# A hybrid attention and DeltaNet layer on one core: scan operands loaded in portions, scales folded into a matrix, pauses in the late modulation

## The chip, the cores and the metric

The kernel runs on one core of a Trainium2 chip. Its engines are TensorE (PE; its weight loads are listed apart as PEld), VectorE (DVE), ScalarE (ACT), GpSimd (POOL) and SyncE (SP), which here only issues transfers. Each engine takes its own instructions in order and waits for the others through semaphores. The metric is the device time of one execution in microseconds (us); lower is better. Times are medians of several runs, and one further run is made under the profiler.

## The reference

One layer over 256 latent tokens and 256 context tokens of width 2048, all in float32. Cut to what matters here:

```python
sh1, sc1, g1, sh2, sc2, g2 = split(silu(c) @ w_ada + b_ada, 6)      # modulation of the latents
p_l = modulate(rmsnorm(x, norm_mix), sh1, sc1) @ w_in               # the same for ctx with c_ctx
k, v = mla_kv(...)      # rmsnorm, w_kv_b; rmsnorm of [k_nope, k_rope] over 192; rotary on k_rope
q = mla_q(...)          # rmsnorm, w_q_b; rmsnorm over 192 with weight q_norm; rotary on the last 64
y_mla = softmax(q @ [k_l, k_c].T * 192**-0.5) @ [v_l, v_c]          # 8 heads
# DeltaNet, per head and direction, 8 chunks of 64: 4 of the context, then 4 of the latents
v_new = u_c - w_c @ s;  s_next = s * g_c + k_c.T @ v_new            # the scan over chunks
o = q_c @ s + a_c @ v_new                                           # latents only
y = sigmoid(ga) * (y_mla @ w_o_mla) + sigmoid(gb) * (y_dn @ w_o_dn)
x = x + g1 * (y @ w_out)
x = x + g2 * conv_glu(modulate(rmsnorm(x, norm_ffn), sh2, sc2), w_ffn_up, ffn_conv, w_ffn_down)
```

The modulation has six parts. The kernel calls the first two early (they are needed at once) and the other four, `g1`, `sh2`, `sc2`, `g2`, late.

## The kernel before, in words

Activations lie transposed, 128 features on the partitions and 256 tokens of a stream along a row. To keep accuracy, a weight tile `raw` (128 x 1024, 512 KB) is split into two halves: `split` lets ACT write the rounded value `whi` (L119) and DVE the rest `wlo` (L120), 512 columns at a time. `mm_hl` then does two matmuls: `whi` against both parts of the activation (512 columns) and `wlo` against its high part (256 columns). There are NR=5 buffers of `raw` and NH=6 pairs of `whi` and `wlo`. All PE work is issued through one helper, so that its rows have line L68.

The stages, with their place in the profiled execution: the early modulation and first projections (0 to 152 us, names `fp`, `amp`); the DeltaNet head inputs (`mmp`, to 441); attention with the gates `wz` and `wgm` as filler (`kps`, `qps`, `sps`, `yps`, `gtp`, to about 757); the scan with the gates `wgd` and the attention's output projection as filler (`kp`, `yp`, `sp_`, `op`, `gtp`, `brp`, to 957); `o_norm` and the second output projection (`obp`, `brp`, to 1036); `wout` (`ops`, to 1127); the gated MLP's up projection (`fps`, to 1630); its down projection (`dps`, to 1874).

**The late modulation** is `ada_rest`, a generator of 128 steps. Each loads a tile `rawa` of 512 KB into the same five `raw` buffers, one step ahead, and lets DVE multiply it with `sch` and sum it (L271). `sch` is one half of silu(c), spread over the partitions and loaded from `Sc` in DRAM into its only buffer at steps 0, 16, 48, 80 and 112. `Side` gives a generator time: a caller adds nanoseconds to what is owed, and the generator runs until the costs that it yields (1300 for a step) have used them up. So its steps are spread over the stages by numbers: ADB in the head inputs, AD in the attention, ADS in the scan, WO for each of the 16 tiles of `wout`, 1000 for each of the 43 tiles of the up projection. Before `wout` the first of the four parts must be done, and after it the third (`while ada.done < 3: ada(1)`), since `h2_tile` needs `adaT` of both; `ada.finish()` stands ahead of the down projection.

**The scan** goes over 8 chunks in the order 4, 5, 6, 7, 0, 1, 2, 3; the last four also give the output. The state `S` depends on the step before: PE `kp`, DVE `r`, PE `yp`, ACT `y`, PE `sp_`, DVE `S`. Its operands are loaded by SP into `jit`, two buffers of each: `kt` (`KTs`), `v` (`Vs`), the inverted system `tt` (six transfers from `Xq` and `Xo`), `ke` (`KEs`). Steps with output load `av` (`As`, two transfers) and `qe` (`QEs`) too, with one buffer each.

**The attention** works on pairs of heads. `k_head` makes the keys `kps`, splits them into `kt` and squares them (`ksq`) for the norm `ks`; `q_tile` makes the queries `qx` and multiplies them by their norm weights; the third tile holds the rotary part, and `rps` multiplies it by the matrix `perm`, which swaps halves.

The scheduler that builds the program may move instructions of an engine against each other where nothing is pinned, so that the written order is not the issued one. Every transfer of SP and ACT takes one of eight completion semaphores in turn and waits for its last user.

Of the kernel before, what the change touches and what calls it, by code (L numbers as in the profile page):

```python
# [8 lines left out]
F32 = mybir.dt.float32  # L9
# [7 lines left out]
P = 128  # L17
# [19 lines left out]
CB = 2000  # L37
CC = 7000
RE = 1.0
ADS = 0.4  # L40
OD = 8000
OC = 4000
WO = 500
IK = 7000
NW = 3
SCP = (2, 5, 7)
# [7 lines left out]
def hybrid_block(ctx: ExitStack, tc: tile.TileContext, io, dbg=None):  # L54
# [136 lines left out]
    def row_bcast(pl, ps, r, n):  # L191

        row_spread(ps, row_diag(pl, r, n), n)

    class Rms:
# [18 lines left out]
        def finish(self, mul, out):  # L214
            n, pl = self.n, self.pl
            ms = pl.tile([P, 4], F32, tag="ms", name="ms", bufs=1)[:, :n]
            dve.tensor_scalar(out=ms, in0=self.ss[:, :n], scalar1=mul, scalar2=EPS, op0=ALU.mult, op1=ALU.add)
            rsq(pl, ms, ms, n)
            bc_ps = psa.tile([P, 512], F32, tag="aux", name="bc_ps")
            row_bcast(pl, bc_ps, ms, n)  # L220
            if out is not None:
                act.copy(out.rearrange("p a b -> p (a b)"), bc_ps[:, : n * P])
            return bc_ps
# [27 lines left out]
    def ada_rest():  # L251


        def load(i):
            w = wr.tile([P, GR], F32, tag="raw", name="rawa", bufs=NR)
            c, n = divmod(i, 32)
            sync.dma_start(w, io["wada2"][c, (n // 16 + c) % 2, n % 16])
            return w

        parts = ad.tile([P, 2, 16], F32, name="parts")  # L260
        half, ahead = None, load(0)
        for i in range(128):
            c, n = divmod(i, 32)
            h, j = (n // 16 + c) % 2, n % 16
            if h != half:
                half, sch = h, ad.tile([P, GR], F32, tag="sch", name="sch")
                sync.dma_start(sch, Sc[h])
            w = ahead
            if i < 127:
                ahead = load(i + 1)  # L270
            dve.tensor_tensor_reduce(out=w, in0=w, in1=sch, scale=1.0, scalar=0.0, op0=ALU.mult, op1=ALU.add, accum_out=parts[:, h, j : j + 1])  # L271
            if n == 31:
                cs = slice(16 * c, 16 * c + 16)
                dve.tensor_tensor(out=adaT[:, cs], in0=parts[:, 0], in1=parts[:, 1], op=ALU.add)
                dve.tensor_tensor(out=adaT[:, cs], in0=adaT[:, cs], in1=bada[:, 32 + 16 * c : 48 + 16 * c], op=ALU.add)
                ada.done = c + 1
            yield 1300
# [632 lines left out]
    dve.tensor_scalar(out=krf[0:64], in0=krd[0:64], scalar1=off["kn_r"][0:64], scalar2=None, op0=ALU.mult)  # L910
    rp = psa.tile([64, T], F32, tag="aux", name="rp")
    pe.matmul(rp, perm[0:64, 0:64], krf[0:64, 0], start=True, stop=True)
    rt = pn.tile([P, T], F32, name="rt")
    dve.tensor_tensor(out=rt[0:64], in0=rp, in1=sinT[0:64], op=ALU.mult)
    dve.tensor_tensor(out=krf[0:64, 0], in0=krf[0:64, 0], in1=cosT[0:64], op=ALU.mult)
# [43 lines left out]
    def mla_project(b):  # L959
# [5 lines left out]
        def k_head(h2):  # L965
            kps = psa.tile([P, 512], F32, tag="aux", name="kps")
            for k in range(4):
                mm3(kps, W(h2 * 512 + k * P), [lat[k][:, n] for n in range(2)], k == 0, k == 3)
            kt = pc2.tile([P, 2, 512], F32R, tag=f"kt{h2}", name="kt")
            split(kps, kt[:, 0], kt[:, 1])  # L970
            ksq = pc2.tile([P, 512], F32, tag="ksq", name="ksq", bufs=1)
            act.activation(ksq, kps, AF.Square)
            kts.append(kt)
            sqs.append(ksq)

# [25 lines left out]
        def q_tile(j):  # L1001
            ps = psa.tile([P, 512], F32, tag="aux", name="qps")
            for k in range(4):
                mm_hl(ps, P, W(j * 512 + k * P), qan_[:, k], k == 0, k == 3)
            qx = pc2.tile([P, T], F32, tag="qx", name="qx")
            gather(ps, P, qx)
            act.activation(qsq[:, j], qx, AF.Square)
            act.activation(qx, qx, AF.Copy, scale=qkn if j < 2 else off["qn_r"])
            return qx

        k_head(0)
# [18 lines left out]
        for _ in sc0:  # L1030
            pass
        for j in range(2):
            qx = q_tile(j)
            split(qx, qts[j][:, 0], qts[j][:, 1])
        for _ in sc1:
            pass
        yield 3500
# [3 lines left out]
        pe.matmul(rps, perm, qx, start=True, stop=True)  # L1041
        rq = ryx[:, 0]
        dve.tensor_tensor(out=rq, in0=rps, in1=sinT, op=ALU.mult)
        dve.tensor_tensor(out=qx, in0=qx, in1=cosT, op=ALU.mult)
        dve.tensor_tensor(out=qx, in0=qx, in1=rq, op=ALU.add)
        for h2 in range(2):
            hs, ls = slice(64 * h2, 64 * h2 + 64), slice(64 - 64 * h2, 128 - 64 * h2)
# [130 lines left out]
    def scan():  # L1178
# [6 lines left out]
        S = ps1.tile([P, HEADS, 2, P], F32, name="S")  # L1185
        steps = (4, 5, 6, 7, 0, 1, 2, 3)

        def load(n):
            st = steps[n]
            kt, ke, v = (jit[:, 2 * j + n % 2].rearrange("p (h c) -> p h c", c=P) for j in range(3))  # L1190
            tt = TTv[n % 2]
            sync.dma_start(kt, KTs[st])
            sync.dma_start(v, Vs[st])
            for d in range(2):
                for r, c, x in ((0, 0, Xq[1]), (32, 32, Xq[2]), (0, 32, Xo)):
                    rs, cs = slice(64 * d + r, 64 * d + r + 32), slice(64 * d + c, 64 * d + c + 32)
                    n = 16 * d + 2 * st
                    sync.dma_start(tt[rs, :, cs], x[n : n + 2].rearrange("a g c i -> c (a g) i"))
            sync.dma_start(ke, KEs[st])
            return kt, ke, v, tt  # L1200

        def load_out(st):
            av = TTv[2]
# [4 lines left out]
            sync.dma_start(qe, QEs[st])  # L1208
            return av, qe

        ahead = load(0)
        yield 0
        for n, st in enumerate(steps):
            kt, ke, v, tt = ahead
            lat, first, last = st < 4, n == 0, n == 7
            if not last:
                ahead = load(n + 1)
            if lat:
                av, qe = load_out(st)
            rs = []  # L1220
            for q in range(2):
                if first:
                    rs.append(v[:, 4 * q : 4 * q + 4])
                    continue
                r = ps1.tile([P, 4, P], F32, tag="r", name="r", bufs=2)
                kp = psa.tile([P, 4, P], F32, tag="aux", name="kp")
                for j in range(4):
                    h = 4 * q + j
                    for d in range(2):
                        hs = slice(64 * d, 64 * d + 64)  # L1230
                        pe.matmul(kp[hs, j], kt[:, h, hs], S[:, h, d], start=True, stop=True)
                    dve.scalar_tensor_tensor(out=r[:, j], in0=kp[:, j], scalar=negc[:, st, h : h + 1], in1=v[:, h], op0=ALU.mult, op1=ALU.add)
                rs.append(r)
            yield CA
            y = ps1.tile([P, HEADS, P], F32, tag="y", name="y")
            for q in range(2):
                h4 = slice(4 * q, 4 * q + 4)
                yp = psa.tile([P, 4, P], F32, tag="aux", name="yp")
                for j in range(4):
                    pe.matmul(yp[:, j], tt[:, 4 * q + j], rs[q][:, j], start=True, stop=True)  # L1240
                act.copy(y[:, h4], yp)
            yield CB
            if lat:
                op = [psm.tile([P, 4, 2, 64], F32, tag="mm", name="op") for q in range(2)]
# [283 lines left out]
```

## Time and profile before

| what | value |
|---|---|
| median of 3 runs | 1875.42 us (1861.37, 1875.42, 1878.97) |
| profiled execution, its own time | 1875.89 us |
| its span, first to last instruction | 1874.0 us |
| granted TensorE clock, mean over the span | 0.983 |
| busy: PE, PEld | 1798.7 us (96%), 1533.5 us (82%) |
| busy: DVE, ACT, POOL | 1379.9 us (74%), 935.1 us (50%), 44.6 us (2%) |
| moved by DMA | 420.23 MB, mean 224 GB/s |
| late modulation on DVE, L271 | 128 instructions, 155.9 us |

The span lies 1.9 us below the execution's own time, which is within half a microsecond of the median. PE is busy nearly all the time, but matmuls are pipelined and the profile models their ends, so that a busy PE may still run slowly, above all where the granted clock is low. The granted clock has two levels, 1.2 and 2.4 GHz; a figure between 0.5 and 1 is a mean over a stretch with both.

### The profile page before, as it was taken

What the parts mean: (1) busy time and instruction counts of PE and PEld (TensorE: products, weight loads), DVE (VectorE), ACT (ScalarE), POOL (GpSimd) and SP (SyncE); (2) the same over time, 40 slices, a digit from 0 to 9 for tenths busy, and PEclk for the clock granted to TensorE, in tenths of its full rate; (3) what the DMA queues carried; (4) which work ended last, traced back from release to release, by engine and by line L of the source; (5) the groups of instructions that cost most, each with busy time, mean ns of one, the idle gap of its engine ahead of it and who ended that gap; (6) DMA issues with size and microseconds to landing.
All of it is one profiled execution on the core that took longest, in us unless ns stands there. A gap on an engine that the chain in (4) does not pass through costs nothing.

```text
span 1874.0 us, 32978 instructions
## 1 busy us (share of the span) xinstructions
PE 1798.7 (96%) x12376; PEld 1533.5 (82%) x12376; DVE 1379.9 (74%) x2777; ACT 935.1 (50%) x1911; POOL 44.6 (2%) x45
## 2 busy tenths in 40 slices
PE   7899999999999998898999997999999999999999
PEld 5788887888888787776878886888888888888888
DVE  5677999879777786566779776878878877755554
ACT  3334554444666565322346556555555555544443
POOL 0000010000000000000000000000000000000000
PEclk9999999999999999889999998999999999999999
DMA  9992788765868777778776774776776766666663
GB/s 353 348 354 75 225 250 247 215 211 144 263 215 261 221 231 228 237 234 286 244 255 227 220 231 146 237 232 217 234 220 219 220 187 188 180 204 197 191 200 121
DMA packets 195153, 420.23 MB, mean 224 GB/s; under 512 B 61297, under 2 KB 101361, under 8 KB 192561
## 3 DMA queue, kind: packets, MB, share of 16 engines
q1 hardware_dynamic: 168096, 402.92, 67.2%
q10 hardware_dynamic: 26896, 15.21, 2.7%
q8 instruction: 97, 1.59, 0.3%
q14 instruction: 64, 0.52, 0.1%
HBM read 389.09 MB, written 28.84 MB: 223 GB/s over the span
## 4 chain that ended last, share of the span: by engine, by line
PE 72%; issue 10%; DMA 8%; DVE 6%; ACT 2%; POOL 1%; SPq 0%; ACTq 0%; POOLq 0%; DVEq 0%
PE fps L68 25%; PE dps L68 13%; PE mmp L68 11%; PE gtp L68 6%; DMA rawa<-in_wada 3%; PE fp L68 3%; PE brp L68 2%; PE op L68 1%; DVE rawa L271 1%; PE kp L68 1%; DVE wlo L120 1%; DMA wt<-in_wadas 1%; PE yp L68 1%; PE kps L68 1%; DMA raw<-in_wgd 1%
## 5 line engine op out<-in xcount | busy, mean ns | idle before, releaser
L119 ACT CAST whi<-raw 128x512 fp32r<-128x512 f32 (+1 forms) x940 | 576.1, 619 | 424.0 <-PE dps L68 114.4
L120 DVE TENSOR_TENSOR wlo<-raw,whi 128x512 fp32r<-128x512 f32 (+1 forms) x940 | 634.1, 686 | 206.3 <-ACT whi L119 198.0
L68 PE MATMUL fps<-H,whi 128*128 128x512 f32 x1376 | 484.7, 400 | 5.3 <-DVE H L120 4.7
L68 PE MATMUL fps<-H,wlo 128*128 128x256 f32 x1376 | 375.1, 282 | 0.5 <-DVE wlo L120 0.5
L68 PEld LDWEIGHTS fps<-H,whi 128*128 128x128 f32 x1376 | 254.9, 189 | 63.9 <-issue 4.9
L68 PEld LDWEIGHTS fps<-H,wlo 128*128 128x128 f32 x1376 | 260.2, 189 | 8.3 <-DVE wlo L120 0.9
L68 PE MATMUL gtp<-h,whi 128*128 128x512 f32 x640 | 235.5, 404 | 7.0 <-ACT whi L119 7.0
L68 PE MATMUL mmp<-h,whi 128*128 128x512 f32 x640 | 228.8, 400 | 0.0
L68 PE MATMUL dps<-GB,whi 128*128 128x512 f32 x560 | 195.9, 391 | 0.0
L271 DVE CUSTOM_DVE_ANT_0 rawa<-rawa,sch 128x1024 f32<-128x1024 f32 x128 | 155.9, 1221 | 52.9 <-DMA rawa<-in_wada 49.8
L68 PE MATMUL gtp<-h,wlo 128*128 128x256 f32 x640 | 176.4, 286 | 0.5 <-DVE wlo L120 0.5
L68 PE MATMUL mmp<-h,wlo 128*128 128x256 f32 x640 | 176.5, 282 | 0.0
L68 PE MATMUL dps<-GB,wlo 128*128 128x256 f32 x560 | 155.1, 282 | 0.0
L68 PEld LDWEIGHTS gtp<-h,whi 128*128 128x128 f32 x640 | 121.2, 191 | 32.3 <-ACT whi L119 7.2
L68 PEld LDWEIGHTS mmp<-h,whi 128*128 128x128 f32 x640 | 119.0, 188 | 25.9 <-ACT dkx L502 0.3
L68 PEld LDWEIGHTS gtp<-h,wlo 128*128 128x128 f32 x640 | 122.0, 191 | 6.2 <-DVE wlo L120 1.2
L68 PEld LDWEIGHTS dps<-GB,whi 128*128 128x128 f32 x560 | 105.1, 188 | 21.9
L68 PEld LDWEIGHTS mmp<-h,wlo 128*128 128x128 f32 x640 | 120.3, 188 | 3.2 <-issue 1.0
L68 PEld LDWEIGHTS dps<-GB,wlo 128*128 128x128 f32 x560 | 105.7, 189 | 0.6
L68 PE MATMUL fp<-h,gh 128*128 128x256 f32 (+1 forms) x448 | 86.3, 292 | 6.2 <-ACT h L68 5.3
L68 PEld LDWEIGHTS fp<-h,gh 128*128 128x128 f32 (+1 forms) x448 | 70.1, 191 | 12.1 <-ACT h L68 6.5
L490 ACT COPY fx<-fps 128x256 f32<-128x256 f32 x86 | 32.0, 374 | 71.6 <-PE fps L68 71.5
(562 smaller groups left out, 2627.9 us busy)
## 6 DMA issues: line engine op xcount, KB each, us to landing
rawa<-in_wada SPq DMA_DIRECT2D x128, 512.0 KB, 4.7
raw<-in_wgate SPq DMA_DIRECT2D x82, 512.0 KB, 4.1
raw<-in_wval SPq DMA_DIRECT2D x82, 512.0 KB, 4.5
raw<-in_wdown SPq DMA_DIRECT2D x80, 512.0 KB, 4.3
wt<-in_wadas SPq DMA_DIRECT2D x16, 1024.0 KB, 8.2
raw<-in_wadab SPq DMA_DIRECT2D x32, 512.0 KB, 7.3
raw<-in_wgm SPq DMA_DIRECT2D x32, 512.0 KB, 5.0
raw<-in_wgd SPq DMA_DIRECT2D x32, 512.0 KB, 5.6
```

The source lines that it names most:

```text
L68: i = f(*a, **k)
L119: act.copy(hi, raw)
L120: dve.tensor_tensor(out=lo, in0=raw, in1=hi, op=ALU.subtract)
L271: dve.tensor_tensor_reduce(out=w, in0=w, in1=sch, scale=1.0, scalar=0.0, op0=ALU.mult, op1=ALU.add, accum_out=parts[:, h, j : j + 1])
L490: act.copy(out, ps[:M, T:])
```

## The change

- `ada_rest`: two pauses of 1300 ahead of each change of `sch` but the first, and four behind each; a pause uses up owed time and issues nothing. The scan gives the steps less time (ADS from 0.4 to 0.3) and `wout` more (WO from 500 to 1500).
- `scan`: the operands of the next step are no longer loaded together at a step's beginning; `kt` and `v` follow the use of `kt`, the system follows `yp`, and `ke` is loaded at the beginning of its own step, behind `av` and `qe`.
- `k_head` squares the keys ahead of the split. `q_tile` writes the two parts of the scaled queries directly, and the rotary tile stays unscaled: `perm` is multiplied by the weights once, and the product with cos takes them along.
- `Rms.finish` spreads the norms with plain matmuls against the identity in place of two rounded diagonal matrices.

```diff
-ADS = 0.4
+ADS = 0.3
-WO = 500
+WO = 1500
...
-            row_bcast(pl, bc_ps, ms, n)
+            for t in range(n):
+                pe.matmul(bc_ps[:, t * P : t * P + P], ms[:, t : t + 1].broadcast_to([P, P]), ident, start=True, stop=True)
...
             if h != half:
+                for _ in range(2 if i else 0):
+                    yield 1300
                 half, sch = h, ad.tile([P, GR], F32, tag="sch", name="sch")
                 sync.dma_start(sch, Sc[h])
+                for _ in range(4):
+                    yield 1300
...
+    dve.tensor_scalar(out=perm, in0=perm, scalar1=off["qn_r"], scalar2=None, op0=ALU.mult)
...
+            ksq = pc2.tile([P, 512], F32, tag="ksq", name="ksq", bufs=1)
+            act.activation(ksq, kps, AF.Square)
             kt = pc2.tile([P, 2, 512], F32R, tag=f"kt{h2}", name="kt")
             split(kps, kt[:, 0], kt[:, 1])
-            ksq = pc2.tile([P, 512], F32, tag="ksq", name="ksq", bufs=1)
-            act.activation(ksq, kps, AF.Square)
...
+            if j < 2:
+                act.activation(qts[j][:, 0], qx, AF.Copy, scale=qkn)
+                dve.scalar_tensor_tensor(out=qts[j][:, 1], in0=qx, scalar=qkn, in1=qts[j][:, 0], op0=ALU.mult, op1=ALU.subtract)
             act.activation(qsq[:, j], qx, AF.Square)
-            act.activation(qx, qx, AF.Copy, scale=qkn if j < 2 else off["qn_r"])
...
-            qx = q_tile(j)
-            split(qx, qts[j][:, 0], qts[j][:, 1])
+            q_tile(j)
...
-        dve.tensor_tensor(out=qx, in0=qx, in1=cosT, op=ALU.mult)
+        dve.scalar_tensor_tensor(out=qx, in0=qx, scalar=off["qn_r"], in1=cosT, op0=ALU.mult, op1=ALU.mult)
...
-        ahead = load(0)
+        kv, tt, ke = load_kv(0), load_system(0), load_ke(0)
...
-            if not last:
-                ahead = load(n + 1)
             if lat:
                 av, qe = load_out(st)
+            if n and not last:
+                ke = load_ke(n)
...
                 rs.append(r)
+            if not last:
+                kv = load_kv(n + 1)
             yield CA
...
                 act.copy(y[:, h4], yp)
+            if not last:
+                tt = load_system(n + 1)
             yield CB
```

What the change moves on SP at the first step of the scan with output. Before, these stand in a row between two filler weights (`raw`):

```order
L267 DMA sch_9808<-Sc_123 128x1024
L257 DMA rawa_9810<-in_wada2 128x1024
L257 DMA rawa_9813<-in_wada2 128x1024
L1192 DMA jit_8894<-KTs_1812 128x1024
L1193 DMA jit_8894<-Vs_1814 128x1024
L1198 DMA jit_8894<-Xq_1818 32x8x32 x2
L1198 DMA jit_8894<-Xo_1819 32x8x32
L1198 DMA jit_8894<-Xq_1818 32x8x32 x2
L1198 DMA jit_8894<-Xo_1819 32x8x32
L1199 DMA jit_8894<-KEs_1813 128x1024
L1206 DMA jit_8894<-As_1820 64x8x64 x2
L1208 DMA qe_9827<-QEs_1815 128x1024
```

And now, with the filler weights among them:

```order
L258 DMA rawa_9723<-in_wada2 128x1024
L1221 DMA jit_8819<-As_1820 64x8x64 x2
L1223 DMA qe_9728<-QEs_1815 128x1024
L1214 DMA jit_8819<-KEs_1813 128x1024
L1199 DMA jit_8819<-KTs_1812 128x1024
L1200 DMA jit_8819<-Vs_1814 128x1024
L125 DMA raw_9769<-in_wgd 128x1024
L258 DMA rawa_9800<-in_wada2 128x1024
L1209 DMA jit_8819<-Xq_1818 32x8x32 x2
L1209 DMA jit_8819<-Xo_1819 32x8x32
```

`sch` is gone from here (it is now loaded in `wout`), and a filler weight stands between the two portions of operands.

On SP at the end of `wout`, the last of its weights and the first of the up projection (`in_wgate`, `in_wval`, halves of 256 KB), before:

```order
L257 DMA rawa<-in_wada 128x1024
L1346 DMA xr<-in_xT 128x512
L125 DMA raw<-in_wout 128x1024 x2
L125 DMA raw<-in_wgate 128x512
L125 DMA raw<-in_wval 128x512
```

And now:

```order
L258 DMA rawa<-in_wada 128x1024
L1366 DMA xr<-in_xT 128x512
L125 DMA raw<-in_wout 128x1024 x2
L258 DMA rawa<-in_wada 128x1024 x11
L125 DMA raw<-in_wgate 128x512
L125 DMA raw<-in_wval 128x512
```

Eleven loads of the late modulation have come in between.

On DVE at the same place, from the last tile of `wout` (`x1`) to the first use of the up projection's norm (`bc_ps`), before:

```order
L1349 SCALAR_TENSOR_TENSOR x1_11800<-yx_12788,adaT_88,xr_12723 128x256
L120 TENSOR_TENSOR wlo_12910<-raw_12907,whi_12909 128x512
L1353 TENSOR_TENSOR ssq_11801<-ssq_11801,x1q_12792 128x256
L217 TENSOR_SCALAR ms_12804<-ss_12795 128x2
L177 CAST rb_h_12808<-ms_12804 128x2
L178 TENSOR_TENSOR rb_l_12809<-ms_12804,rb_h_12808 128x2
L183 TENSOR_TENSOR rb_d_12812<-ident_75,rb_h_12808 128x256
L183 TENSOR_TENSOR rb_d_12814<-ident_75,rb_l_12809 128x256
L1369 TENSOR_TENSOR h2_12849<-bc_ps_12807,x1_11800 128x256
```

And now, down to the first weights of the up projection, which come ahead of `h2`:

```order
L1373 TENSOR_TENSOR ssq_11699<-ssq_11699,x1q_12710 128x256
L277 ISA rawa_12740,parts_2171<-rawa_12740,sch_12208 128x1024
L277 ISA parts_2171 128x1
L217 TENSOR_SCALAR ms_12757<-ss_12748 128x2
L280 TENSOR_TENSOR adaT_88<-parts_2171 128x16
L281 TENSOR_TENSOR adaT_88<-adaT_88,vecs_86 128x16
L277 ISA rawa_12743,parts_2171<-rawa_12743,sch_12208 128x1024
L277 ISA parts_2171 128x1
L1384 SCALAR_TENSOR_TENSOR a2_12763<-adaT_88,vecs_86 128x16
L120 TENSOR_TENSOR wlo_12773<-raw_12770,whi_12772 128x512
```

The norm `ms` and the factor `a2` now stand behind steps of the late modulation, and the first `wlo` of the up projection behind `a2`.

## Rows read from the trace of the kernel before

**Rows 1.** Stages: us, busy PE, PEld, DVE, ACT, POOL; PEclk, DMA share, GB/s.

```profile
516.00:723.00 207.00, 196.81 (x1453) 170.61 (x1453) 157.99 (x348) 131.37 (x305) 11.11 (x9) 0.98 0.74 233
...
757.00:957.00 200.00, 186.12 (x1249) 151.57 (x1249) 130.38 (x313) 59.13 (x122) 0.00 (x0) 0.94 0.75 252
...
1036.00:1127.00 91.00, 90.30 (x515) 78.53 (x513) 69.12 (x131) 49.37 (x97) 0.00 (x0) 1.00 0.71 226
1127.00:1165.00 38.00, 28.97 (x145) 23.29 (x145) 23.69 (x56) 22.03 (x48) 0.70 (x1) 0.82 0.49 150
1165.00:1630.00 465.00, 464.08 (x2629) 402.88 (x2628) 369.75 (x720) 255.61 (x501) 0.00 (x0) 1.00 0.68 213
```

**Rows 2.** PE in order of time, at waits after 460 us (in brackets).

```profile
475.37 0.59 PE L68 MATMUL ks<-ones,ksq 128*32 128x1 f32 x32 [2.13 <-ACT ksq L972]
...
532.61 0.43 PE L68 MATMUL ks<-ones,ksq 128*32 128x1 f32 x32 [1.88 <-ACT ksq L972]
...
641.86 0.70 PE L68 MATMUL rps<-qx,rope 128*128 128x256 f32 x2 [4.37 <-ACT qx L1008]
...
864.68 0.80 PE L68 MATMUL gtp<-h,whi 128*128 128x512 f32 x1 [7.00 <-ACT whi L119]
...
1135.21 0.77 PE L68 MATMUL fps<-H,whi 128*128 128x512 f32 x1 [2.49 <-DVE H L120]
```

**Rows 3.** Windows of 5 us around waits, columns as in the first group.

```profile
835.00:840.00 5.00, 5.00 (x20) 3.25 (x21) 4.33 (x9) 0.00 (x0) 0.00 (x0) 0.50 0.35 107
...
860.00:865.00 5.00, 0.32 (x1) 0.29 (x1) 0.34 (x1) 0.99 (x2) 0.00 (x0) 0.62 0.97 361
865.00:870.00 5.00, 5.00 (x21) 4.04 (x21) 4.68 (x9) 1.84 (x5) 0.00 (x0) 0.70 1.05 366
```

**Rows 4.** SP in order of time, 838 to 859 us.

```profile
838.70 0.42 SPq L267 DMA_DIRECT2D sch<-Sc  x1
...
840.28 5.65 SPq L257 DMA_DIRECT2D rawa<-in_wada  x2
...
855.31 0.30 SPq L1198 DMA_DIRECT2D jit<-Xo  x1
...
858.22 0.38 SPq L125 DMA_DIRECT2D raw<-in_wgd  x1
```

**Rows 5.** What SP waited for, 735 to 985 us: total, times, longest.

```profile
SPq L1206 <- PE op L68: 5.2, 1, 5.2
```

**Rows 6.** The chain of waits, in the scan: start, us, what.

```profile
762.65 5.65 PE gtp L68 x32
```

**Rows 7.** ACT in order of time, at a key square and a rotary query.

```profile
531.17 0.81 ACT L1079 ACTIVATE s__6359<-s__6359,mns,qm 128x512 f32<-128x512 f32 x1 [2.23 <-DVE mns L1078]
...
531.99 0.57 ACT L972 ACTIVATE ksq<-kps 128x512 f32<-128x512 f32 x1
...
641.30 0.51 ACT L1008 ACTIVATE qx<-qx,vecs 128x256 f32<-128x256 f32 x1
```

**Rows 8.** DVE in order of time, 638 to 641 us.

```profile
638.91 1.23 DVE L271 CUSTOM_DVE_ANT_0 rawa<-rawa,sch 128x1024 f32<-128x1024 f32 x1 [3.08 <-DMA rawa<-in_wada]
...
640.06 0.42 DVE L491 TENSOR_TENSOR qx<-qps,qx 128x256 f32<-128x256 f32 x1
```

**Rows 9.** The page: late modulation on DVE, and its loads (us to landing).

```profile
L271 DVE CUSTOM_DVE_ANT_0 rawa<-rawa,sch 128x1024 f32<-128x1024 f32 x128 | 155.9, 1221 | 52.9 <-DMA rawa<-in_wada 49.8
...
rawa<-in_wada SPq DMA_DIRECT2D x128, 512.0 KB, 4.7
```

**Rows 10.** SP in order of time, at the end of wout.

```profile
1110.74 0.33 SPq L125 DMA_DIRECT2D raw<-in_wgate  x1
```

**Rows 11.** DVE in order of time, from the norm after wout to h2.

```profile
1130.08 0.16 DVE L217 TENSOR_SCALAR ms<-ss 128x2 f32<-128x2 f32 x1 [0.43 <-PE ss L68]
...
1131.05 0.17 DVE L177 CAST rb_h<-ms 128x2 fp32r<-128x2 f32 x1 [0.81 <-POOL ms L171]
...
1132.76 0.76 DVE L1369 TENSOR_TENSOR h<-bc_ps,x 128x256 f32<-128x256 f32 x2 [0.68 <-PE bc_ps L68]
```

More of the change, by code (lines that the diff above doesn't have):

```diff
@@ L1186, in scan, with load_kv, load_system @@
         steps = (4, 5, 6, 7, 0, 1, 2, 3)
[L1188 to L1193, printed above, removed]
+        def load_kv(n):
+            kt, v = (jit[:, 2 * j + n % 2].rearrange("p (h c) -> p h c", c=P) for j in (0, 2))
+            sync.dma_start(kt, KTs[steps[n]])
+            sync.dma_start(v, Vs[steps[n]])
+            return kt, v
+        def load_system(n):
+            st, tt = steps[n], TTv[n % 2]
             for d in range(2):
@@ L1198, in load, with load_ke @@
                     sync.dma_start(tt[rs, :, cs], x[n : n + 2].rearrange("a g c i -> c (a g) i"))
-            sync.dma_start(ke, KEs[st])
-            return kt, ke, v, tt
+            return tt
+        def load_ke(n):
+            ke = jit[:, 2 + n % 2].rearrange("p (h c) -> p h c", c=P)
+            sync.dma_start(ke, KEs[steps[n]])
+            return ke
         def load_out(st):
@@ L1209, in load_out @@
             return av, qe
-        ahead = load(0)
+        kv, tt, ke = load_kv(0), load_system(0), load_ke(0)
         yield 0
         for n, st in enumerate(steps):
-            kt, ke, v, tt = ahead
+            kt, v = kv
             lat, first, last = st < 4, n == 0, n == 7
-            if not last:
-                ahead = load(n + 1)
             if lat:
                 av, qe = load_out(st)
+            if n and not last:
+                ke = load_ke(n)
             rs = []
```

## The prediction, made before the change ran

> **What bounds the kernel now.** I read the windows by stage first. PE is busy for 96% of the span, so the question is where it is not, or runs slowly. In the up projection it is busy for 464.08 of 465 us and in `wout` for 90.30 of 91, both at a granted clock of 1.00 [rows 1]; nothing done there to DVE, ACT or SP can shorten these, only lengthen them. Three stretches have something to give: the attention (196.81 of 207 us, clock 0.98), the scan (186.12 of 200, clock 0.94) and the passage from `wout` to the up projection (28.97 of 38, clock 0.82).
>
> Next I read PE in order of time for its waits [rows 2]. Two of the longer ones in the attention are for the key squares (2.13 and 1.88 us), one is for the rotary query (4.37). The scan's longest is 7.00 us at 864.68, for a filler weight. The last row is the start of the up projection: `wout` ends at 1127 [rows 1], so the passage costs 8.2 us before any matmul of the new stage. The clock adds to this. In the two windows around the 7.00 us wait it is 0.62 and 0.70 [rows 3], part 1.2 and part 2.4 GHz, which takes another 5 x 0.38 + 5 x 0.30 = 3.4 us; a full window at 0.50 stands at 835. What PE waits for it then pays for once more.
>
> **The scan's operands.** The 7.00 us wait comes from SP. Between 838.70 and 858.22 SP issues no filler weight [rows 4]: `sch`, two `rawa` that sit in the queue until 845.9 for lack of a free buffer, then `kt`, `v`, six pieces of the system (the last only at 855.31, since the eight completion semaphores are all in use), `ke`, `av`, `qe`, and at last `in_wgd`. By the order, some 4.1 MB stand between two weights; at the 361 GB/s of this window [rows 3] that is 11.4 us, while PE uses up the two weights of a gate tile in 5.65 us [rows 6]. Afterwards `sch` is gone from here, the six pieces come behind a weight, and 0.5 (`rawa`) + 0.26 + 4 x 0.52 = 2.9 MB, or 8.0 us, remain in a row, with five buffers ahead of them. I take the wait and most of its clock as gone: **-9 us**, of at most 7.0 + 3.4. The other rows bound it. If PE lost nothing at all in the scan, neither the 200 - 186.1 = 13.9 us in which it is not busy nor the 0.06 x 200 = 12 us of its clock [rows 1], it would be -26. The other end: `av` and `qe`, which have one buffer, now stand ahead of `ke`, `kt` and `v`, and SP has waited 5.2 us for PE's `op` at that place [rows 5]; all of that behind PE would cost +5, against part of the gain: +3.
>
> How the clock behaves is the Trainium skill's "TensorE: Matmul & The Clock Gate", section on HAM oscillation: after a wait of some length matmuls start slowly, once for each such wait. The rows agree here (7.00 us, then 0.62 and 0.70). By the rule the scan's wait is worth 10.4 us, without it 7.0.
>
> **The attention.** ACT loses 12 operations of up to 0.51 us [rows 7], one a query tile, and DVE's products gain some 0.06 us each; ACT is busy for 131 of 207 us, so this alone is worth nothing. What counts is the order of the waits. The first pair's `ks` now has 40 gate matmuls ahead of it in PE's order where it had 23; 17 more at 0.353 us a pair [rows 6] are 3 us, and the 2.13 us go. The second pair's `ksq` still stands behind the exponential that waits 2.23 us for DVE [rows 7]: ACT's order has moved `kt` behind it rather than `ksq` ahead. Those 1.88 us stay. The 4.37 us before `rps` are mostly DVE, which waits 3.08 us for a `rawa` and only then makes `qx`, at 640.06 [rows 8]; what the change removes is from its end at 640.48 to 641.86, or 1.4 us, and the order takes back 0.9, since five matmuls that stood ahead of `rps` are now behind it. With the steps that leave (next) I take **-4**, between -11 (all waits of this stage down to the level of the best) and +3 (a new order that fits worse; nothing excludes it).
>
> **The late modulation.** By SP's order the 128 steps were spread 21, 49, 28, 6 and 24 over head inputs, attention, scan, `wout` and the rest; now 17, 36, 21, 23 and 31. A step is 1.22 us of DVE, 4.7 us from issue to landing, and DVE waited 49.8 us in all for them [rows 9]. The 20 steps that leave attention and scan are in the terms above. In the head inputs PE is full: 0, within 1.
>
> In `wout`, 12 of the 23 lie among the tiles in place of 6. DVE has 91 - 69.1 = 21.9 us idle there [rows 1]; six more at 1.22 us and a wait of 1.4 (49.8 us in 36 waits) take 16. That hides them, barely: **+1**, from 0 to +4.
>
> The other eleven stand in one row behind the last `wout` weight. Ahead of them SP reaches that place at 1110.74 [rows 10]. They are 5.77 MB, 16.0 us at 361 GB/s. Nine must pass DVE before `ms`, the tenth before `a2`, and the first weights of the up projection land behind all eleven. With 4.7 us for the first and 1.45 for each further one, the ninth is there at 1127.1, ahead of `ms` at 1130.08 [rows 11]: no delay. The eleventh lands at 1130, four half weights at 2.9 us more, 1133; DVE splits the last at about 1134.5 and makes `h2` some 3 us later than the present 1132.76. The shorter spread of the norm (four DVE operations from 1131.05 on, one matmul pair) gives about 1 us, but `h2` no longer waits for it. Before, the six pairs of split buffers could be filled ahead of 1135; now DVE and ACT split them while they make `h2`, which PE waits for: 2 us. **+5**, between -1 (only the shorter spread counts) and +16 (the whole row lies on the path).
>
> Five more stand in a row at the end of the up projection, ahead of the first `in_wdown`: 2.6 MB, 7.3 us at that rate. Five raw buffers and three split ones are in front of PE, at 2.8 us each (half of [rows 6]); **+0.5**, from 0 to +4.
>
> **The sum.** -9 - 4 + 1 + 5 + 0.5 = -6.5 us on the profiled execution's 1875.9, which is half a microsecond from the median of the runs: **1869**.
>
> **Rivals.** *The row of eleven decides* (slower): the change pays in one place, at once and at PE's cost. It does if the row starts later than 1127 - 16.0 = 1111.0, that is if `wout`, now with twice the steps among its tiles, holds SP up for more than 0.3 us there. For: SP's buffers are shared with the weights, and PE has no slack in `wout`. Against: the same buffers come free faster behind a step than behind a weight. All 16 us on the path, +4 in `wout`, and the scan's gain without its clock: 1875.9 + 16 + 4 - 7 - 4 = 1885; without any gain in the scan 1892 and, with +4 at the end, 1896.
>
> *The scan gets all of PE* (faster): the portions end not one wait but all of them. For: half of what PE loses there is clock, which follows its waits. Against: `kp`, `r` and the state's update follow each other through DVE whatever the loads do. With -26 for -9: 1852.
>
> *The loads do not change what is late*: the bytes are the same, and a weight behind them waits as long, at another step. By the Trainium skill's "DMA: Bandwidth & Descriptors", section on queues, rings and completion order, each DMA engine takes the descriptors of a queue in order, so that a weight issued behind a portion has to wait for it. In rows: the wait of 7.00 moves, the attention keeps its 4, the passage costs 5: 1875.9 - 4 + 1 + 5 = 1878. The 11.4 against 8.0 us of transfers in a row speak against it.
>
> **How the numbers follow.** I give the forecast 0.60 (1860 to 1880), the row of eleven 0.15, the full scan 0.13, loads that change nothing 0.12. About 1% (18.8 us) is what a measurement of this kernel can tell from no change; its three runs lie 0.9% apart. Faster than 1857 is the full scan and the forecast's own tail, 0.03: 0.16. Slower than 1894 is the worse half of the row of eleven and a little for an order that I misread: 0.09. The rest, 0.75, is within 1%. The range reaches into both outer cases: 1850 to 1887.
>
> **What would show it.** Right: no wait above 3 us in the scan, and PE busy for more than 190 of 200 us there at a clock above 0.96; the `ks` wait at 475 gone and that near 532 still there; the first `fps` 10 to 13 us behind the last `ops`; `wout` and the up projection as long as before. Wrong: a wait for `kt`, `ke` or `qe` in the scan, `raw<-in_wgate` landing after 1140 relative to the present clock, or PE short of weights inside `wout`. My weakest number is +5: it leans on a transfer rate read from one window.

## The result, and the profile after

The changed kernel takes 1859.45 us (median of 9 runs, 1854.68 to 1862.83) against 1870.37 us for the kernel before (9 runs, 1860.85 to 1878.97): a ratio of 0.9948, 95% interval 0.9928 to 0.9967. That is some 10 us less, where -6.5 was forecast. The profiled spans are 1858.6 and 1874.0 us. The profiled execution of before was itself a long one: in a later comparison 29 runs of that kernel lay between 1857.72 and 1876.45 us, so some of the 15 us between the two traces is chance. Much of that chance is the granted clock: the fastest of these runs had a mean of 0.989, the slowest 0.978; the two profiled executions had 0.983 (before) and 0.990 (after).

First the windows by stage, columns as in [rows 1], with bounds at the first instruction of each stage. Of before: attention, scan, `wout`, the passage from the last `ops` to the first `fps`, and the 30.4 us behind that, in which PE works while `h2` is made.

```profile
460.40:750.00 289.60, 272.22 (x1975) 234.97 (x1975) 216.89 (x463) 182.14 (x416) 17.42 (x15) 0.98 0.76 235
750.00:973.80 223.80, 206.10 (x1488) 168.32 (x1488) 145.59 (x344) 72.92 (x152) 3.00 (x1) 0.94 0.76 256
1036.10:1127.30 91.20, 90.50 (x514) 78.43 (x512) 69.26 (x131) 49.37 (x97) 0.00 (x0) 1.00 0.71 225
1127.30:1135.20 7.90, 1.25 (x19) 0.81 (x19) 4.32 (x13) 3.00 (x7) 0.70 (x1) 0.72 0.33 97
1135.20:1165.60 30.40, 28.02 (x128) 22.88 (x128) 19.57 (x45) 19.63 (x43) 0.00 (x0) 0.85 0.53 165
```

The same five stages of after, and the rest of the up projection:

```profile
460.60:741.50 280.90, 270.30 (x1993) 234.39 (x1993) 207.12 (x441) 180.22 (x408) 16.76 (x15) 0.99 0.72 221
741.50:953.30 211.80, 199.41 (x1480) 162.47 (x1480) 136.49 (x327) 71.80 (x149) 2.90 (x1) 0.99 0.75 250
1017.40:1107.30 89.90, 89.90 (x513) 78.33 (x511) 73.87 (x138) 45.91 (x91) 0.00 (x0) 1.00 0.82 278
1107.30:1124.60 17.30, 1.62 (x20) 1.26 (x21) 15.02 (x34) 6.07 (x13) 0.69 (x1) 0.62 0.84 288
1124.60:1155.00 30.40, 29.36 (x149) 24.36 (x150) 23.62 (x55) 23.57 (x52) 0.00 (x0) 0.94 0.59 184
1155.00:1614.60 459.60, 459.57 (x2606) 399.41 (x2605) 370.37 (x722) 249.68 (x490) 0.00 (x0) 1.00 0.69 221
```

The attention is 8.7 us shorter and the scan 12.0. The passage is 9.4 longer, with DVE busy for 15.02 of its 17.30 us. Of that about 5 come back: the up projection, from the first `fps` to the first `dps`, takes 490.2 us instead of 495.0.

The scan's gain has to be read with the clock. Where the scan of before ran at 1.2 GHz, in order of time, all of it:

```profile
755.40:762.20 6.80, 6.80 (x30) 5.90 (x28) 0.00 (x0) 1.85 (x4) 0.00 (x0) 0.50 0.92 296
782.60:786.00 3.40, 3.40 (x17) 2.58 (x16) 3.24 (x8) 0.00 (x0) 0.00 (x0) 0.51 0.18 13
830.40:840.70 10.30, 9.90 (x41) 6.39 (x42) 6.24 (x15) 1.14 (x2) 0.00 (x0) 0.50 0.46 152
861.20:864.70 3.50, 0.02 (x1) 0.02 (x1) 0.04 (x1) 0.69 (x2) 0.00 (x0) 0.50 0.99 376
864.70:868.00 3.30, 3.30 (x9) 2.57 (x10) 3.18 (x6) 1.59 (x3) 0.00 (x0) 0.50 1.03 417
```

And in the scan of after:

```profile
773.50:776.90 3.40, 3.40 (x15) 2.78 (x15) 3.17 (x7) 0.00 (x0) 0.00 (x0) 0.50 0.48 167
```

Only the last two rows of before belong to the 7.00 us wait, and in the first of these PE is idle; 20.1 us of PE's work at 1.2 GHz lie elsewhere. A pair of matmuls on a weight takes 0.64 us at that level (839.40 to 840.04) and 0.35 at 2.4 GHz (843.24 to 843.59), so that about 0.45 us is lost in each microsecond of work there. By this estimate some 9 of the scan's 12.0 us are clock: 23.4 us of work at 1.2 GHz in before against 3.4 in after.

PE in order of time in after, at its waits (in brackets), against [rows 2]:

```profile
479.60 0.43 PE L68 MATMUL ks<-ones,ksq 128*32 128x1 f32 x32 [1.85 <-ACT ksq L978]
...
637.90 0.70 PE L68 MATMUL rps<-qx,rope 128*128 128x256 f32 x2 [2.18 <-DVE qx L497]
...
846.05 0.50 PE L68 MATMUL brp<-YM,whi 128*128 128x512 f32 x1 [2.38 <-ACT whi L119]
...
904.53 0.50 PE L68 MATMUL brp<-YM,whi 128*128 128x512 f32 x1 [1.97 <-ACT whi L119]
...
1115.93 0.40 PE L68 MATMUL ss<-ones,ssq 128*32 128x1 f32 x16 [8.64 <-DVE ssq L1373]
...
1124.61 0.76 PE L68 MATMUL fps<-H,whi 128*128 128x512 f32 x1 [5.46 <-DVE H L120]
```

The 7.00 us wait of the scan is gone; two new ones, of 2.38 and 1.97 us, are for weights of the output projection (`brp`). Both come from ACT's order. In after, ACT in order of time:

```profile
843.70 0.37 ACT L496 COPY zx<-gtp 128x256 f32<-128x256 f32 x1 [4.13 <-PE gtp L68]
...
845.38 3.74 ACT L119 CAST whi<-raw 128x512 fp32r<-128x512 f32 x7 [0.40 <-ACT zx L861]
```

The `whi` that `brp` needs stands behind the copy of a gate tile, which can only start when that tile's last matmul is done; PE has nothing else in between.

DVE in after, in the passage:

```profile
1111.29 1.23 DVE L277 CUSTOM_DVE_ANT_0 rawa<-rawa,sch 128x1024 f32<-128x1024 f32 x1
...
1112.44 0.42 DVE L497 TENSOR_TENSOR yx<-ops,yx 128x256 f32<-128x256 f32 x1
1112.78 1.22 DVE L277 CUSTOM_DVE_ANT_0 rawa<-rawa,sch 128x1024 f32<-128x1024 f32 x1
...
1113.92 0.48 DVE L1369 SCALAR_TENSOR_TENSOR x<-yx,adaT,xr 128x256 f32<-128x256 f32 x1
1114.32 1.22 DVE L277 CUSTOM_DVE_ANT_0 rawa<-rawa,sch 128x1024 f32<-128x1024 f32 x1
...
1115.46 0.42 DVE L1373 TENSOR_TENSOR ssq<-ssq,x1q 128x256 f32<-128x256 f32 x1
```

Steps of the late modulation stand between the three operations of the last `wout` tile and run back to back. The last matmul ended at 1107.3; the tile's `yx` comes five microseconds later.

### The profile page after: what moved, and what is told of

Same layout as the page of the kernel before. It is cut to its first block, busy times and chain, and to the rows that moved or that the text cites. A ratio compares the mean times of both kernels' runs of the same rounds, so it can differ in the third digit from the quotient of the medians.

```text
span 1858.6 us, 32954 instructions
## 1 busy us (share of the span) xinstructions
PE 1788.5 (96%) x12386; PEld 1527.4 (82%) x12386; DVE 1376.6 (74%) x2766; ACT 928.4 (50%) x1899; POOL 44.3 (2%) x45
## 4 chain that ended last, share of the span: by engine, by line
PE 54%; DMA 3%; DVE 2%; ACT 1%; issue 1%; POOL 0%; SPq 0%; ACTq 0%; DVEq 0%
PE fps L68 26%; PE dps L68 13%; PE brp L68 5%; PE gtp L68 4%; PE ops L68 3%; DMA rawa<-in_wada 2%; PE op L68 1%; PE kp L68 1%; PE yp L68 1%; DVE wlo L120 1%; DMA raw<-in_wgate 0%; DMA jit<-Vs 0%; DVE rawa L277 0%; DMA yraw<-Ys 0%; DVE S L1284 0%
```

## The experiments

All ratios are to the kernel before, with 95% intervals. Lengths of stages are from the first instruction of one name to that of the next on PE: attention from `kps` to `yp`, scan from `yp` to `obp`, `wout` over `ops`, passage to `fps`, up projection to `dps`; "wait" is PE's longest in the scan ahead of `obp`, without the one that ends with the first `yp` (up to 2.7 us); "low" is the time in the scan in which PE worked at 1.2 GHz, and "at 2.4" the scan less 0.45 of it, the estimate from above. Ratios come from several runs, everything else from one trace of each kernel.

| kernel | ratio | attention | scan | wait | low | at 2.4 | wout | passage | up |
|---|---|---|---|---|---|---|---|---|---|
| before | 1 | 289.6 | 223.9 | 7.00 | 23.4 | 213.4 | 91.1 | 7.9 | 495.0 |
| after | 0.9948 | 280.9 | 211.8 | 2.38 | 3.4 | 210.3 | 89.9 | 17.3 | 490.2 |
| scan_only | 0.9982 | 280.1 | 218.8 | 2.38 | 13.7 | 212.6 | 89.9 | 7.9 | 494.3 |
| mod_only | 0.9919 | 276.3 | 206.2 | 0.84 | 6.8 | 203.1 | 89.9 | 16.9 | 490.0 |
| mod_again (the same) | 0.9919 | 278.4 | 209.3 | 0.84 | 13.1 | 203.4 | 89.9 | 16.7 | 490.6 |
| att_only | 1.0003 | 280.3 | 223.7 | 5.91 | 30.7 | 209.9 | 90.6 | 7.9 | 494.7 |
| norm_only | 0.9991 | 285.6 | 230.5 | 6.35 | 43.8 | 210.8 | 89.9 | 7.5 | 493.2 |
| no_scan | 0.9928 | 282.9 | 210.5 | 0.84 | 16.6 | 203.0 | 89.9 | 17.0 | 489.9 |
| mod_scan | 0.9929 | 277.4 | 213.3 | 2.38 | 10.0 | 208.8 | 89.9 | 15.8 | 491.5 |
| numbers_only | 0.9937 | 280.8 | 211.0 | 0.84 | 17.1 | 203.3 | 92.7 | 9.9 | 493.3 |
| steps_in_scan | 0.9995 | 279.6 | 218.6 | 6.32 | 14.2 | 212.2 | 95.4 | 12.8 | 493.8 |
| mod_no_row | 0.9928 | 277.3 | 207.9 | 0.84 | 10.2 | 203.3 | 96.3 | 10.1 | 491.6 |
| light_row | 0.9944 | 280.7 | 214.4 | 2.38 | 9.9 | 209.9 | 89.9 | 11.8 | 494.9 |
| row_without_loads | 0.9933 | 281.6 | 213.5 | 2.38 | 6.6 | 210.5 | 89.9 | 13.1 | 491.3 |

**One part at a time.** scan_only makes these edits of `scan` alone:

```diff
-            if not last:
-                ahead = load(n + 1)
+            if n and not last:
+                ke = load_ke(n)
...
+            if not last:
+                kv = load_kv(n + 1)
...
+            if not last:
+                tt = load_system(n + 1)
```

> The kernel before with the scan's operands in portions and nothing else; the modulation's 28 steps and one sch stay in the scan. Theory (the order of the loads is what PE waited for): the 7.00 us wait goes, no wait of the scan is above 3 us, the scan is 9 to 12 us shorter than 223.8 us and the whole 8 to 12 us shorter, all other stages within 1 us. Rival (the scan's 12 us come from the seven steps and the sch that left it): the wait of some 7 us stays and the whole is within 3 us of before.

Ratio 0.9982 (0.9964 to 1.0000). The 7 us wait goes, but two waits of 2.38 us for `brp` weights come, and the scan is 5 us shorter than in before, not 9 to 12. Both theories miss the size; the first has the mechanism of the wait. By the estimate the scan is no shorter at equal clock (212.6 us against 213.4): what the portions save at the wait they lose elsewhere.

mod_only makes the edits of the late modulation alone:

```diff
-ADS = 0.4
+ADS = 0.3
-WO = 500
+WO = 1500
...
+                for _ in range(2 if i else 0):
+                    yield 1300
...
+                for _ in range(4):
+                    yield 1300
```

> The kernel before with the late modulation's pauses and the two numbers ADS and WO alone. Theory: the attention loses 4 us (13 steps leave), the scan at most 4 of its 12 (sch and seven steps leave, the row of operands stays, so a wait of 4 to 6 us stays), the passage to the up projection costs 9 more and about 5 come back right behind it; sum -4, between -8 and 0. Rival (the steps alone carry the gain of the whole change): scan at 212 us, whole 10 us shorter. Second rival (it only pays the passage): attention and scan as before, whole 4 us longer.

Ratio 0.9919 (0.9891 to 0.9947), scan 206.2 us. The first rival holds: these edits carry the gain of the whole change, and the operands loaded in one row cost PE nothing once they are made. My theory of the loads falls here.

att_only makes the edits of keys and queries alone:

```diff
+            ksq = pc2.tile([P, 512], F32, tag="ksq", name="ksq", bufs=1)
+            act.activation(ksq, kps, AF.Square)
...
-            act.activation(qx, qx, AF.Copy, scale=qkn if j < 2 else off["qn_r"])
...
+    dve.tensor_scalar(out=perm, in0=perm, scalar1=off["qn_r"], scalar2=None, op0=ALU.mult)
```

> The kernel before with the edits of keys and queries alone (squares ahead of the split, weights in perm, the parts of the queries written at once). Theory: 4 of the 8.7 us by which the attention became shorter are here (the wait before rps from 4.37 to about 2.2, one of the waits for ks of about 2 us gone), whole 2 to 5 us shorter. Rival (the 13 modulation steps that left are all of it): attention and whole within 1.5 us of before.

Ratio 1.0003 (0.9984 to 1.0021): nothing. Its attention of 280.3 us is no evidence, since scan_only has 280.1 with the code of before: the 289.6 us of the profile before lie at the long end of what one kernel shows there.

norm_only makes the edit of `Rms.finish` alone:

```diff
-            row_bcast(pl, bc_ps, ms, n)
+            for t in range(n):
+                pe.matmul(bc_ps[:, t * P : t * P + P], ms[:, t : t + 1].broadcast_to([P, P]), ident, start=True, stop=True)
```

> The kernel before with the norms spread by plain matmuls alone. Theory: it costs or saves where PE waits for a norm and nowhere else: about 1 us less in the passage to the up projection, whole within 2 us of before. Rival (it is what made the head inputs 4 us longer in the changed kernel, by another order there): first gtp of the attention at 445 rather than 441 us, whole 3 to 4 us longer.

Ratio 0.9991 (0.9973 to 1.0009), passage 7.5 us in place of 7.9, head inputs as long as in before (289.8 us; 289.7 before). It is worth nothing that can be measured, and the rival is out.

**One part undone.** no_scan is the changed kernel with the `scan` of before (the first diff above, the other way).

> The changed kernel with the scan's operands loaded together, as before. Theory (once sch and seven steps have left the scan, the portions are not needed and bring the two waits of some 2 us for brp weights): scan at about 206 us rather than 211.8, no wait in it above 2.3 us, whole about 5 us shorter than the changed kernel (0.990 to 0.993 of before). Rival (the portions earn their 5 us here as they do alone): scan at 216 us or more with a wait of 5 us or more, whole about 5 us longer than the changed kernel (0.997 to 1.000 of before).

Ratio 0.9928 (0.9902 to 0.9955); scan at 210.5 us, and no wait above 0.84 in it ahead of `obp`. So the portions do not earn anything here. What they cost needs more than one profile, and mod_scan gives the second pair. It is mod_only with the portions.

```diff
 (mod_only, and)
+                kv = load_kv(n + 1)
+                tt = load_system(n + 1)
```

> The kernel before with the modulation edits (pauses, ADS 0.3, WO 1500) and the scan's portions. Theory (the portions remove a wait that the modulation edits have removed already): attention and scan together within 4 us of the 482.5 us that the modulation edits alone gave, whole 0.990 to 0.994 of before. Rival (the portions add two waits of 2 us for brp weights and clock behind them): attention and scan together at 488 us or more, whole 0.994 to 0.998 of before.

Ratio 0.9929 (0.9902 to 0.9955), attention and scan together 490.7 us, with the waits of 2.38 and 1.97 us back: by the stages the rival holds, by the ratio the theory, and the ratio's interval reaches over both. Over all profiles with the pauses and ADS at 0.3, the scan takes 206.2, 209.3, 207.9 and 210.5 us without portions and 211.8, 214.4, 213.5 and 213.3 with them: means 208.5 and 213.2, and no overlap. At equal clock the groups stand further apart: 203.0 to 203.4 us and 208.8 to 210.5. The two `brp` waits, 4.4 us together (4.8 in scan_only), are in the five kernels with portions and in no other; what else slows PE there was not traced. The runs agree: each run's time multiplied by its granted clock, a rough estimate of its time at 2.4 GHz, has medians of 1826, 1829 and 1826 us in mod_only, mod_again and no_scan, of 1834 and 1835 in mod_scan and after, and of 1837 to 1838 in before. In mod_only, ACT's order has the `brp` weight ahead of the gate tile:

```profile
837.37 1.14 ACT L119 CAST whi<-raw 128x512 fp32r<-128x512 f32 x2 [1.67 <-DMA raw<-in_womla]
...
839.66 0.37 ACT L495 COPY zx<-gtp 128x256 f32<-128x256 f32 x1 [0.30 <-PE gtp L68]
```

**Which number.** numbers_only has ADS 0.3 and WO 1500 without the pauses, so that `sch` stays in the scan; steps_in_scan has the pauses and ADS 0.4, so that most steps stay there and `sch` leaves. As run, DVE does 28 steps in the scan of before, 21 in numbers_only and mod_only, and 26 in steps_in_scan.

```diff
 numbers_only: before, and
-ADS = 0.4
+ADS = 0.3
-WO = 500
+WO = 1500
 steps_in_scan: mod_only, and
-ADS = 0.3
+ADS = 0.4
```

> The kernel before with ADS at 0.3 and WO at 1500 and without the pauses: 22 steps and sch stay in the scan, 22 stand among the wout tiles, one behind them. Theory (it is sch at that place of the queue, moved away by the pauses, that PE waited for): a wait of 5 us or more for a filler weight stays in the scan, scan at 217 to 222 us, passage 8 us, wout 2 to 5 us longer than 91, whole 0.995 to 0.999 of before. Rival (the number of steps in the scan): no wait above 3 us in the scan, scan at 206 to 210 us, whole 0.989 to 0.993 of before.

> The kernel before with the pauses and WO at 1500, but ADS left at 0.4: 28 steps in the scan as before, sch behind it, 20 steps among the wout tiles and a row of three behind them. Theory (sch's place and not the number of steps decides in the scan, and the row costs the passage): scan at 206 to 211 us, passage of about 10 us, up projection 2 to 4 us longer than with the row of eleven, whole 0.988 to 0.993 of before. Rival (seven more steps bring the wait back): a wait of 4 us or more in the scan, scan at 215 us or more, whole 0.995 or more of before.

Ratios 0.9937 (0.9913 to 0.9961) and 0.9995 (0.9979 to 1.0012). Both times the rival holds, with numbers_only just outside its ranges (scan 211.0 us for 206 to 210, 0.9937 for at most 0.993): with 21 steps and `sch` there is no wait above 0.84 us ahead of `obp`, with 26 steps and no `sch` one of 6.32. The number of steps decides, since ADS alone differs between steps_in_scan and mod_only. Of the 15 us between steps_in_scan (median 1868.68 us) and mod_again (1853.28), the scan has 9 to 12 and the stages from `wout` to the up projection 5. PE's wait in steps_in_scan:

```profile
848.36 0.80 PE L68 MATMUL gtp<-h,whi 128*128 128x512 f32 x1 [6.32 <-ACT whi L119]
```

SP in order of time, ahead of the row of operands, first of steps_in_scan (first `yp` at 738.1), then of numbers_only (742.9):

```profile
826.83 2.51 SPq L257 DMA_DIRECT2D rawa<-in_wada  x2
...
840.45 0.38 SPq L125 DMA_DIRECT2D raw<-in_wgd  x1
```

```profile
827.23 0.33 SPq L257 DMA_DIRECT2D rawa<-in_wada  x1
...
840.01 0.38 SPq L125 DMA_DIRECT2D raw<-in_wgd  x1
...
849.38 0.42 SPq L267 DMA_DIRECT2D sch<-Sc  x1
...
864.15 0.38 SPq L125 DMA_DIRECT2D raw<-in_wgd  x1
```

In numbers_only `sch` comes one step of the scan later than in before: there it stands with two `rawa` and all operands in one row between the weights issued at 847.86 and 864.15, and PE does not wait behind that row. The first stretch without a filler weight is about as long in both kernels; but from the first `yp` the next weight is issued at 102.3 us in steps_in_scan and at 97.1 in numbers_only. Every `rawa` takes one of the five buffers of the weights, so I read this as the weights' lead being used up by the steps; which of buffer and order does it was not tried apart.

**The row of eleven.** light_row is the changed kernel with steps 85 to 95 at 64 of their 1024 columns; row_without_loads keeps them full and drops the loads of steps 86 to 96. DVE's order stays the same but for neighbours.

```diff
 light_row
+            m = 64 if 84 < i < 96 else GR
-            dve.tensor_tensor_reduce(out=w, in0=w, in1=sch, scale=1.0, scalar=0.0, op0=ALU.mult, op1=ALU.add, accum_out=parts[:, h, j : j + 1])
+            dve.tensor_tensor_reduce(out=w[:, :m], in0=w[:, :m], in1=sch[:, :m], scale=1.0, scalar=0.0, op0=ALU.mult, op1=ALU.add, accum_out=parts[:, h, j : j + 1])
 row_without_loads
+            if not 85 < i < 97:
                 sync.dma_start(w, io["wada2"][c, (n // 16 + c) % 2, n % 16])
-            dve.tensor_tensor_reduce(out=w, in0=w, in1=sch, scale=1.0, scalar=0.0, op0=ALU.mult, op1=ALU.add, accum_out=parts[:, h, j : j + 1])
+            dve.tensor_tensor_reduce(out=w, in0=sch if 85 < i < 97 else w, in1=sch, scale=1.0, scalar=0.0, op0=ALU.mult, op1=ALU.add, accum_out=parts[:, h, j : j + 1])
```

> The changed kernel, with steps 85 to 95 of the late modulation multiplying only 64 of their 1024 columns (the rest of these sums is left out); their loads stay. Theory (the row of eleven delays the last wout tile through the order of DVE, 1.2 us for each step in front): passage of 8 to 11 us rather than 17.3. Rival (it is the transfers of the row, as the prediction priced it): passage still 15 to 17 us, with DVE idle in it, waiting for rawa.

> The changed kernel without the loads of steps 86 to 96 of the late modulation: these steps multiply sch by itself at full width (their 11 loads are left out, and these sums are other numbers). Theory (DVE's order): the steps can run earlier, in DVE's idle time of wout, but those that stand between the last tile's operations still cost 1.2 us each: passage 11 to 16 us. Rival (the transfers): passage of 8 to 10 us.

Passages of 11.8 and 13.1 us: of the 9.4 us that the row adds, 5.5 go with DVE's work and 4.2 with the transfers. The first lies just outside its theory's 8 to 11, the second inside 11 to 16; so both limits lie close together. DVE of light_row, with the same three operations of the last tile, now waits for the transfers:

```profile
1108.62 0.23 DVE L278 CUSTOM_DVE_ANT_0 rawa<-rawa,sch 128x64 f32<-128x64 f32 x1 [0.82 <-DMA rawa<-in_wada]
...
1109.91 0.23 DVE L278 CUSTOM_DVE_ANT_0 rawa<-rawa,sch 128x64 f32<-128x64 f32 x1 [1.05 <-DMA rawa<-in_wada]
...
1110.06 0.42 DVE L498 TENSOR_TENSOR yx<-ops,yx 128x256 f32<-128x256 f32 x1
```

A transfer comes every 1.29 us here, against 1.48 to 1.54 us for a step and one operation of the tile in after. The totals say more than the passage: light_row's up projection is at 494.9 us again, so that passage and up projection together take 506.7, as in after (507.5; before 502.9). Without the loads it is 504.5. So of the 4.6 us that the row costs in sum, the transfers hold 3.0 and DVE's work 0.8, in one trace each.

mod_no_row is mod_only with steps enough among the tiles that almost no row is left (by SP's order 24 loads stand among the `wout` weights and two behind them):

```diff
-WO = 1500
+WO = 2600
```

> The kernel before with the modulation's pauses and ADS as changed, and WO at 2600, so that all steps of the third part fall among the wout tiles and none stands in a row behind them. Theory (the row costs 9 us in the passage, of which about 5 come back in the up projection): passage back to 8 us, the up projection 4 to 5 us longer than with the row (494 to 495 us), wout at most 2 us longer, whole 1 to 5 us shorter than with WO 1500. Rival (steps between the weights hold them up): wout 4 us or more longer, whole as with WO 1500 or longer.

Ratio 0.9928 (0.9907 to 0.9950). The passage falls from 16.9 to 10.1 us and `wout` grows from 89.9 to 96.3: the rival holds, and the steps cost as much among the tiles as behind them. Their number alone does not decide: by SP's order 12 cost nothing in the changed kernel, where they stand in two groups with twelve weights between, and 5.5 us in steps_in_scan, where they follow each other behind every second weight; 18 cost 2.8 us in numbers_only.

mod_again is mod_only once more:

> The kernel before with the modulation edits alone, once more, beside the other runs of this call. Both theories of the modulation edits: 0.989 to 0.994 of before, attention and scan together at 480 to 487 us. If it is above 0.994, the lead of this version over the changed kernel was chance.

Ratio 0.9919 (0.9892 to 0.9946), medians 1853.28 and, in the first comparison, 1850.78 us. It is the fastest version by its median. It is faster than before; its lead over the changed kernel is not shown, since the intervals overlap and the two did not run side by side. For it speak the 5 us of the scan above, and the times at equal clock.

## Why the prediction was right in its sum and wrong in its parts

The time came out 10 us lower where 6.5 were forecast, within the range. That the sum came near is in part luck: in these traces most of the scan's gain is clock, and the row's cost is what is left of two larger numbers that were not forecast. The terms:

- **The scan, -9.** The size came near by luck (12.0 between the two traces, some 9 of them clock), the cause was wrong. "Afterwards `sch` is gone from here, the six pieces come behind a weight" priced the row of operands by its bytes. That step failed: numbers_only has that whole row with `sch`, mod_only has it without, and neither has the wait; steps_in_scan takes `sch` out and has 6.32 us. What decides is the number of steps, which I had put down as part of "the terms above" without a price of its own. The portions alone remove the wait too, and behind the steps they cost about 5 us (6 to 7 at equal clock), in part by ACT's new order. The bound of +3, from SP waiting for PE's `op`, was the wrong place for that cost.
- **The clock in that term, 3.4.** Over half of it was charged twice: in the window from 860 to 865 [rows 3] PE is busy for only 0.32 us, so that the low clock there costs next to nothing beyond the wait itself. By the rows above, PE works at 1.2 GHz for 3.3 us behind the wait and loses 0.45 x 3.3 = 1.5 us; the wait is worth 8.5 us, not 10.4. What the clock gave back in after came from the other stretches, which were not in the sum. Nor do they follow the long wait from kernel to kernel: steps_in_scan has the wait and 14.2 us of work at 1.2 GHz, numbers_only has no such wait and 17.1. What sets them off was not tried. By the Trainium skill's "TensorE: Matmul & The Clock Gate", section on HAM oscillation, matmuls start slowly after a wait. The trace agrees for this wait: the clock fell during it, and the matmuls from 864.7 to 868.0 ran at 1.2 GHz.
- **The attention, -4.** The wait for `ks` that should go stayed (1.85 us at 479.60), the one near 532 that should stay went, and that for `rps` became 2.2 us shorter, where 1.4 was forecast. None of this needs the edits: mod_only, without them, has 1.89 us for the first `ks`, no wait near 532 and 2.85 for `rps`. And the edits of keys and queries earn nothing: together with the stretch ahead of it (first `gtp` to first `kps`, 15.3 us in after and 18.8 in mod_only), the attention takes 296.2 us in after and 295.1 in mod_only. As far as one trace each can tell, the gain goes with the 13 steps that left: 295.1 to 298.4 us in the five kernels with pauses and without those edits, 300.1 in numbers_only, and 308.8, 299.4, 301.7 and 300.2 in before, scan_only, norm_only and att_only.
- **`wout` with 12 steps, +1:** nothing, as long as in scan_only. **Five at the end, +0.5:** nothing; the down projection takes 239.7 us in both. **Head inputs, 0:** 293.7 us against 289.7; the kernels with pauses have 290.1 to 293.7, those without 289.1 to 289.8, so that the pauses seem to cost up to 4 us there; why was not tried.
- **The row of eleven, +5.** Passage +9.4, up projection -4.8: +4.6. The sum is right by luck, and the step "the ninth is there at 1127.1, ahead of `ms` at 1130.08 [rows 11]: no delay" is the one that failed. It timed the transfers against the norm, and took the last tile's operations to be ahead of the row. DVE has them inside it, at 1.5 us a step, and SP issued the first `in_wgate` 5.3 us behind the last matmul (1112.55), where [rows 10] has it 16.6 us ahead. What comes back I had not priced at all: weights and `h2` are further along when PE starts, and the clock in the next 30.4 us is 0.94 rather than 0.85.

Of the signs that the prediction named, no wait above 3 us in the scan and a clock above 0.96 there came true (0.99). PE was busy for 188 of 200 us there, not 190, the first `fps` stood 17.3 us behind the last `ops`, not 10 to 13, and the two `ks` waits changed places.

Of the rivals, the row of eleven did not decide, the scan did not get all of PE (199.41 of 211.80 us), and "the loads do not change what is late" was nearer to the truth about the portions than the forecast. By the intervals, an edit that is worth 2 or 3 us can't be told from nothing by the runs; of these the stages alone speak, and they hold for one execution each.

## What to carry to other kernels

Where one wait has several candidates in the queue ahead of it, price each as if it alone were removed; here the bytes of the row were the visible ones, and the number of filler steps decided. Where the clock is to be priced with a wait, list every stretch of the stage at the lower level first: most of it may lie away from the wait, and what lies inside the wait costs nothing more. After moving filler work, read the order of the elementwise engine at the next stage boundary: what stands between the last tile's own operations lengthens that passage. Then read the passage and the next stage together, since part of it comes back there: a cure that shortens the passage alone (light_row) may gain almost nothing. Where two edits remove the same wait, it is gained once, and the side effects of both are paid.

## What the hardware showed that I had not expected

The scan's time at 1.2 GHz moves more than its waits: PE worked at that level for 3.4 to 43.8 us of it, and in before, att_only and norm_only, whose `scan` is the same code, for 23.4, 30.7 and 43.8. In before the longest stretch (10.3 us from 830.4) begins behind small matmuls of the state (`kp`) with waits of 0.47 to 0.60 us between them. The same kernel's runs differ by 1% (1857.72 to 1876.45 us), and the granted clock goes with it (0.989 to 0.978, where 0.011 of 1866 us is 20). One stage, the attention, lay between 280.1 and 289.6 us in three profiles whose code there is the same but for a norm's spread. In the row, one transfer of 512 KB every 1.29 us (light_row) is 406 GB/s by this core alone, and the window from 1110 to 1115 us of after shows 402, more than the 361 GB/s that the prediction took from one window.
